# Recurrence: the two directions of a head pair as one product with a block-diagonal T

## The chip, the core and the metric

The kernel runs on one NeuronCore of a Trainium2 chip. The metric is the device time of one execution in microseconds (us), taken as the median of several runs. The engines, by the names of the profile, are PE (TensorE: products, with PEld for its weight loads), DVE (VectorE), ACT (ScalarE), POOL (GpSimd) and SP (SyncE, which here only issues DMAs).

## The reference, cut to what matters

One layer over 512 latent and 256 context tokens of width 1024: a modulated norm, an input projection into a recurrent mixer and a gating MLP, their merge, then 32 experts of which each token takes four. The change lies in the recurrent mixer (RWKV-7, 8 heads of 64, both directions). Per direction and head a 64x64 state goes through the tokens:

```python
def step(S, inp):
    r_t, w_t, k_t, v_t, a_t, b_t = inp
    sa = jnp.einsum('bhvk,bhk->bhv', S, a_t)
    S = S * w_t[:, :, None, :] + sa[..., None] * b_t[:, :, None, :] + v_t[..., None] * k_t[:, :, None, :]
    return S, (jnp.einsum('bhvk,bhk->bhv', S, r_t) if emit else None)
...
for d, rev in enumerate((False, True)):
    ...
    S_c, yc = wkv_scan(S0, rc, dc[d]['w'], dc[d]['k'], vc, dc[d]['a'], dc[d]['b'], rev, ctx_out)
    ...
    _, yl = wkv_scan(S_c, rl, dl[d]['w'], dl[d]['k'], vl, dl[d]['a'], dl[d]['b'], rev, True)
```

The context scan starts from zero, the latent scan from its last state; the two directions are summed for the latent tokens.

## The kernel before

**Chunks.** The recurrence isn't run token by token. Tokens are taken in 12 chunks of 64 (4 of context, 8 latent), and heads in 4 pairs p = 0 to 3, so there are 48 steps n = 12 p + i. In a step both directions (d = 0 forward, d = 1 backward) and both heads of the pair (par = 0, 1) are computed. Within a chunk the term sa of a token depends on those before it; this triangular system is solved ahead, once for each chunk, and its inverse T (64x64 for each direction and head) is stored in TT, a tile of 128x24x64: partitions 0 to 63 hold direction 0, partitions 64 to 127 direction 1, and column block 8 sb + 4 par + i % 4 is that of a chunk and head.

**Ahead of the chain.** For the next pair, while this one runs, `pre` (L682 to L724) makes decayed keys and queries, `solve_ab` (L770 to L775) the matrices of the systems, `solve_sub` (L792, L793, on DVE) solves their 32x32 blocks, and `solve_join` joins them (L816 to L824 on PE) and writes the last parts of TT (L825 on ACT, L826 on DVE). The dictionary `todo` in `rwkv` says after which step each of these parts is written into the program. They share the PSUM tag "pre" with two buffers, as `pre_bonus` and `readout` do.

**A step.** `chain_prep(p, i)` prepares operands that don't depend on the state: keys scaled on ACT (L846), turned on PE (L847) and copied back (L848, BKt), the values turned (L852) and copied into one half of UV (L853, L854), queries put into a zero-padded tile on ACT (L869, ARz), masked products with the keys (L873 on PE, L875 on DVE). Then up to two units of `fill` come, each six products of 128x128 by 512 columns (L1094) of the merge gates, which have nothing to do with the recurrence. Then `chain(p, i)`: products L893 and L896 into PSUM (tag "ch", two buffers), copy to Xs on DVE (L898), the product with T (L903), its result copied into the other halves of UV, on ACT (L904) for direction 0 and on DVE (L905) for direction 1; from UV the new state (L914 on PE, L918 or L920 on DVE, with the decayed old state from L911 on POOL), and for latent chunks the output (L927, L931, then L936 or L938 into the tile ysum). UV has two buffers, used in turn.

**The gates.** Each of 16 gates is four units of fill; FILLA gives the steps 2, 1, 1, 2, 1, 1, ... units. A gate ends with a tanh on ACT (L1099) into gt, L1100 on POOL, and for the last eight a product on POOL (L1104) with ybi, a tile of the pool W2 with one buffer, loaded by SP (L1089, L1090); then a store (L1102 or L1105). gt has one buffer.

**The readout.** After the last step of a pair `readout` (L940 to L969) centres ysum with a product (L950, L951), squares it on ACT (L953) into sq, sums that (L955), takes a root on ACT (L956) and reciprocals on DVE (L958), and scales ysum (L962 to L964 on POOL in the first three pairs). sq has the tag "gsq" with one buffer of its own.

**Order.** Each engine works through its own queue in order. In this part the framework plans the queues: it goes by the order of the program and by when operands and buffers are free, so that an instruction may stand ahead of ones that come before it in the program. The experts (from some 720 us on) keep an order written out by hand.

Of the kernel before, what the change touches and what calls it, by code (L numbers as in the profile page):

```python
# [7 lines left out]
F32 = mybir.dt.float32  # L8
# [147 lines left out]
class K:  # L156
# [671 lines left out]
    def chain_prep(self, p, i):  # L828

        nc = self.nc  # L830
        W = self.W2
        G = self.P[p]
        sb = i // 4
        AR, BK = G["AR", sb], G["BK", sb]
        ch = (i % 4, 3 - i % 4)
        S = G["step", i] = {}
        gc = 3 - i if sb == 0 else 15 - i
        S["f"] = f = (G["F"][:, 0, i + 1:i + 2], G["F"][:, 1, gc:gc + 1]) if i < 11 else None
        bk = S["BKt"] = W.tile([128, 2, 128], F32, name="BKt", bufs=2)
        uv = S["UV"] = self.UV[i % 2]  # L840
        pt = self.psC.tile([128, 4, 128], F32, name="prep")
        if f:

            bf = W.tile([128, 2, 128], F32, name="BKf", bufs=1)
            for d in range(2):
                nc.scalar.activation(bf[:, d, :], BK[:, d, ch[d], :], AF.Copy, scale=f[d])  # L846
                nc.tensor.transpose(pt[:, d, :], bf[:, d, :], self.ident)  # L847
            nc.scalar.copy(bk, pt[:, 0:2])  # L848
        for d in range(2):

            t = self.tok0(sb, d) + 64 * ch[d] + 64 * d
            nc.tensor.transpose(pt[:, 2 + d, :], G["v"][:, t:t + 128], self.ident)  # L852
        nc.scalar.copy(uv[64:128, 0], pt[64:128, 2])  # L853
        nc.scalar.copy(uv[0:64, 1], pt[0:64, 3])  # L854
        mm0 = self.psC.tile([128, 2, 512], F32, name="mm")
        if sb == 0:
            AK = S["AK"] = W.tile([128, 2, 64], F32, name="AK")
            for par in range(2):
                r = slice(64 * par, 64 * par + 64)
                nc.tensor.matmul(mm0[64:128, par, 0:64], BK[r, 0, ch[0], 64:128], AR[r, 0, ch[0], 0:64], start=True, stop=True)  # L860
                nc.tensor.matmul(mm0[0:64, par, 0:64], BK[r, 1, ch[1], 0:64], AR[r, 1, ch[1], 0:64], start=True, stop=True)
            nc.vector.tensor_mul(AK, mm0[:, :, 0:64], self.cst[:, C_MSKC:C_MSKC + 64].rearrange("p (a t) -> p a t", a=1).to_broadcast([128, 2, 64]))
        else:

            AZ = W.tile([128, 2, 2, 128], F32, name="ARz", bufs=1)
            a0, a1 = AR[:, 0, ch[0], :], AR[:, 1, ch[1], :]
            both = bass.AP(tensor=a0.tensor, offset=a0.offset, ap=[list(a0.ap[0]), [a1.offset - a0.offset, 2], [1, 128]])
            for par in range(2):
                nc.scalar.activation(AZ[:, :, par, :], both, AF.Copy, scale=self.cst[:, C_BLK + 64 * par:C_BLK + 64 * par + 1])  # L869
            mm = mm0[:, 0, :].rearrange("p (d a t) -> p d a t", d=2, a=2)  # L870
            MM = S["MM"] = W.tile([128, 2, 2, 128], F32, name="MM", bufs=2)
            for d in range(2):
                nc.tensor.matmul(mm[:, d].rearrange("p a t -> p (a t)"), BK[:, d, ch[d], :], AZ[:, d].rearrange("p a t -> p (a t)"), start=True, stop=True)  # L873
            msk = self.cst[:, C_MSK:C_MSK + 256].rearrange("p (d a t) -> p d a t", d=2, a=1)
            nc.vector.tensor_mul(MM, mm, msk.to_broadcast([128, 2, 2, 128]))  # L875

    def chain(self, p, i):
        nc = self.nc
        W = self.W2
        G = self.P[p]  # L880
        sb = i // 4
        AR, TT = G["AR", sb], G["TT"]
        S = G["step", i]
        ch = (i % 4, 3 - i % 4)
        St, Sn = self.S[(i + 1) % 2], self.S[i % 2]
        uv, bk = S["UV"], S["BKt"]
        xp = self.psC.tile([128, 2, 64], F32, name="ch", bufs=2)
        for par in range(2):
            for d in range(2):

                r = slice(0, 128) if sb > 0 else slice(64, 128) if d == 0 else slice(0, 64)
                ak = S["AK"][r, par, :] if sb == 0 else S["MM"][:, d, par, 0:64]
                nc.tensor.matmul(xp[64 * d:64 * d + 64, par, :], ak, uv[r, d, 64 * par:64 * par + 64], start=(par == 0), stop=(i == 0 and par == 1))  # L893
        if i > 0:
            for d in range(2):
                nc.tensor.matmul(xp[64 * d:64 * d + 64].rearrange("p a b -> p (a b)"), AR[:, d, ch[d], 0:64], St[:, d, :], start=False, stop=True)  # L896
        Xs = W.tile([128, 2, 64], F32, name="Xs", bufs=2)
        nc.vector.tensor_copy(Xs, xp)  # L898
        up = self.psC.tile([128, 2, 64], F32, name="ch", bufs=2)
        for par in range(2):  # L900
            for d in range(2):
                r = slice(64 * d, 64 * d + 64)
                nc.tensor.matmul(up[r, par, :], TT[r, 8 * sb + 4 * par + i % 4, :], Xs[r, par, :], start=True, stop=True)  # L903
        nc.scalar.copy(uv[0:64, 0].rearrange("p (b v) -> p b v", b=2), up[0:64])  # L904
        nc.vector.tensor_copy(uv[64:128, 1].rearrange("p (b v) -> p b v", b=2), up[64:128])  # L905
        if i < 11:
            f = S["f"]
            if i > 0:
                FS = W.tile([128, 2, 128], F32, name="FS", bufs=2)
                for d in range(2):  # L910
                    nc.gpsimd.tensor_scalar(FS[:, d, :], St[:, d, :], f[d], None, op0=OP.mult)  # L911
            sp = self.psC.tile([128, 2, 128], F32, name="ch", bufs=2)
            for d in range(2):
                nc.tensor.matmul(sp[:, d, :], bk[:, d, :], uv[:, d, :], start=True, stop=True)  # L914
            for par in range(2):
                r = slice(64 * par, 64 * par + 64)
                if i == 0:
                    nc.vector.tensor_copy(Sn[r, :, r], sp[r, :, r])  # L918
                else:
                    nc.vector.tensor_add(Sn[r, :, r], sp[r, :, r], FS[r, :, r])  # L920
        if sb > 0:
            MM = S["MM"]
            if i == 4:
                G["y"] = W.tile([128, NLAT], F32, name="ysum")
            yp = self.psC.tile([128, 2, 64], F32, name="ch", bufs=2)
            for d in range(2):
                nc.tensor.matmul(yp[:, d, :], St[:, d, :], AR[:, d, ch[d], 64:128], start=(d == 0), stop=False)  # L927
            for d in range(2):
                for par in range(2):
                    r = slice(64 * par, 64 * par + 64)  # L930
                    nc.tensor.matmul(yp[r, d, :], uv[:, d, r], MM[:, d, par, 64:128], start=False, stop=(d == 1))  # L931
            for d in range(2):
                t = self.tok0(sb, d) + 64 * ch[d] - 256
                o = G["y"][:, t:t + 64]
                if sb == 1:
                    nc.scalar.copy(o, yp[:, d])  # L936
                else:
                    nc.vector.tensor_add(o, o, yp[:, d])  # L938

    def readout(self, p):  # L940

        nc = self.nc
        W = self.W2
        G = self.P[p]
# [4 lines left out]
        ps = self.psR.tile([128, 512], F32, name="pre", bufs=2)  # L949
        nc.tensor.matmul(ps, blk, y, start=True, stop=True)  # L950
        nc.vector.scalar_tensor_tensor(y, ps, -1.0 / 64, y, op0=OP.mult, op1=OP.add)  # L951
        sq = W.tile([128, 512], F32, name="gsq")
        nc.scalar.activation(sq, y, AF.Square)  # L953
        ps = self.psR.tile([128, 512], F32, name="pre", bufs=2)
        nc.tensor.matmul(ps, blk, sq, start=True, stop=True)  # L955
# [16 lines left out]
    def rwkv(self, fill):  # L972
        nc = self.nc
        todo = {}
        self.UV = []
        for j in range(2):
            t = self.W2.tile([128, 2, 128], F32, name=f"UV{j}")
            nc.gpsimd.memset(t, 0.0)
            self.UV.append(t)
        for q in range(1, 4):  # L980
            a = 12 * (q - 2)
            work = [(at, lambda q=q, sb=sb: self.pre(q, sb)) for sb, at in enumerate(PRE if q > 1 else PRE1)]
            work.append((S_END, lambda q=q: self.pre_end(q)))
            work += [(S_AB + sb, lambda q=q, sb=sb: self.solve_ab(q, sb)) for sb in range(3)]
            work += [(S_SUB + i, lambda q=q, i=i: self.solve_sub(q, 31 * i // NSUB, 31 * (i + 1) // NSUB)) for i in range(NSUB)]
            work += [(S_SUB + NSUB + h, lambda q=q, h=h: self.solve_join(q, h)) for h in range(2)]
            work.append((S_BON, lambda q=q: self.pre_bonus(q)))
            for at, f in work:
                todo.setdefault(a + at, []).append(f)
        for n in range(48):  # L990
            p, i = n // 12, n % 12
# [1125 lines left out]
```

## Time and profile before

| | us |
|---|---|
| runs | 1987.66, 1989.9, 1995.83 |
| median | 1989.9 |
| profiled execution, device time | 1995.05 |
| its span, first to last instruction | 1993.3 |
| PE busy in the span | 1903.4 (95%) |
| DVE busy | 1703.8 (85%) |
| ACT busy | 1246.2 (63%) |
| POOL busy | 567.5 (28%) |
| mean granted clock of PE | 0.977 of 2.4 GHz |

The span is divided by the page into 40 slices of 49.8 us. The recurrence lies in slices 7 to 14, some 308 to 678 us. A product's time in the trace goes from its first column to the end of its way through the array, and consecutive products overlap; so an engine that the table calls busy may still have room. In the timeline a row may stand for several instructions of one line (x8), with the start of the first and the time they cover together.

### The profile page before, as it was taken

The page shows a single profiled execution, that of the slowest core. Times are in us where ns is not written, and L with a number is a line of the kernel's source. Part 1 is how long each engine was busy: PE and PEld are TensorE (multiplying, and loading weights), DVE is VectorE, ACT ScalarE, POOL GpSimd, SP SyncE. Part 2 cuts the span into 40 slices and gives each one's busy share as a digit, 9 for nine tenths or more (in the row PEclk, how much of TensorE's full clock was granted, in tenths as well). Part 3 has the DMA queues.
Part 4 walks back from the last instruction along what each step waited for, and adds up shares of the span by engine and source line. Part 5 has one row for each costly group of instructions (what it writes and reads, how often), then busy time and mean ns, then how long its engine had stood idle before and what let it go on. Part 6 is the DMA issues. An engine that isn't in the chain of part 4 may idle for free.

```text
span 1993.3 us, 28998 instructions
## 1 busy us (share of the span) xinstructions
PE 1903.4 (95%) x11136; PEld 1485.9 (75%) x11136; DVE 1703.8 (85%) x1764; ACT 1246.2 (63%) x1441; POOL 567.5 (28%) x423
## 2 busy tenths in 40 slices
PE   7999988989999898999999999999999999999996
PEld 4767766767676688777888887887878878878874
DVE  5755785877776568899999999999999999999996
ACT  4522535454545435777777777777777777777773
POOL 0000516343433364522131131221321311312212
PEclk9999989998989998999999999999999999999998
DMA  9665223120112375999999999999999999999994
GB/s 323 207 202 191 88 94 116 41 81 20 50 43 72 126 246 206 340 354 359 375 364 360 368 367 367 369 365 375 367 359 373 367 363 369 364 371 372 347 383 141
DMA packets 153122, 530.58 MB, mean 266 GB/s; under 512 B 16112, under 2 KB 77296, under 8 KB 103825
## 3 DMA queue, kind: packets, MB, share of 16 engines
q1 hardware_dynamic: 140343, 495.85, 67.0%
q0 software_dynamic: 10272, 26.94, 5.8%
q10 hardware_dynamic: 2362, 5.87, 0.8%
q8 instruction: 90, 1.47, 0.3%
q14 instruction: 55, 0.45, 0.1%
HBM read 500.48 MB, written 36.08 MB: 269 GB/s over the span
## 4 chain that ended last, share of the span: by engine, by line
PE 69%; DVE 7%; issue 3%; POOL 3%; DMA 2%; ACT 1%; SPq 0%; POOLq 0%; DVEq 0%; ACTq 0%
PE dn L1505 6%; PE dn L1504 6%; PE dn L1509 6%; PE up L1504 6%; PE up L1505 6%; PE up L1509 6%; PE gp L1505 6%; PE gp L1504 6%; PE gp L1509 6%; PE fill L1094 2%; PE b L1594 1%; PE b L1553 1%; PE mm L873 1%; PE ch L914 1%; PE acc L166 1%
## 5 line engine op out<-in xcount | busy, mean ns | idle before, releaser
L1493 DVE TENSOR_TENSOR wl<-raw,wh 128x2048 fp32r<-128x2048 f32 x384 | 928.0, 2461 | 1.9 <-issue 1.0
L1487 ACT CAST wh<-raw 128x2048 fp32r<-128x2048 f32 x384 | 721.3, 1905 | 80.7 <-PE gp L1505 65.7
L1540 POOL DMA_INDIRECT xg<-d_h,slots x30 | 35.1, 1171 | 687.0 <-PE b L1553 679.1
L1504 PE MATMUL dn<-wh,aH 128*128 128x512 f32 x512 | 208.3, 407 | 0.7 <-ACT aH L1597 0.7
L1505 PE MATMUL dn<-wh,aL 128*128 128x512 f32 x512 | 206.4, 403 | 0.3 <-DVE aL L1598 0.2
L1504 PE MATMUL up<-wh,xH 128*128 128x512 f32 x512 | 206.2, 403 | 0.0
L1504 PE MATMUL gp<-wh,xH 128*128 128x512 f32 x512 | 205.3, 401 | 0.0
L1505 PE MATMUL up<-wh,xL 128*128 128x512 f32 x512 | 203.0, 397 | 0.0
L1505 PE MATMUL gp<-wh,xL 128*128 128x512 f32 x512 | 202.9, 396 | 0.0
L1612 POOL TENSOR_TENSOR y<-y,mH 128x1024 f32<-128x1024 f32 x31 | 135.8, 4381 | 152.0 <-ACT y L1611 152.0
L1509 PE MATMUL dn<-wl,aH 128*128 128x512 f32 x512 | 140.5, 396 | 0.7 <-DVE wl L1493 0.7
L1509 PE MATMUL up<-wl,xH 128*128 128x512 f32 x512 | 139.7, 394 | 0.0
L1509 PE MATMUL gp<-wl,xH 128*128 128x512 f32 x512 | 139.4, 394 | 0.0
L1597 ACT CAST aH<-b 128x512 fp32r<-128x512 f32 x64 | 37.6, 587 | 144.1 <-PE b L1594 144.1
L1505 PEld LDWEIGHTS dn<-wh,aL 128*128 128x128 f32 x512 | 96.8, 189 | 32.6 <-DVE aL L1598 13.4
L1509 PEld LDWEIGHTS dn<-wl,aH 128*128 128x128 f32 x512 | 96.6, 189 | 24.1 <-DVE wl L1493 1.1
L1509 PEld LDWEIGHTS gp<-wl,xH 128*128 128x128 f32 x512 | 96.1, 188 | 23.6
L1509 PEld LDWEIGHTS up<-wl,xH 128*128 128x128 f32 x512 | 96.6, 189 | 22.7
L1504 PEld LDWEIGHTS up<-wh,xH 128*128 128x128 f32 x512 | 96.5, 189 | 22.6
L1505 PEld LDWEIGHTS up<-wh,xL 128*128 128x128 f32 x512 | 96.8, 189 | 21.6
L1505 PEld LDWEIGHTS gp<-wh,xL 128*128 128x128 f32 x512 | 96.4, 188 | 21.6
L1504 PEld LDWEIGHTS gp<-wh,xH 128*128 128x128 f32 x512 | 96.3, 188 | 21.4
(524 smaller groups left out, 3851.4 us busy)
## 6 DMA issues: line engine op xcount, KB each, us to landing
raw<-in_exp_w_gate_dram SPq DMA_DIRECT2D x128, 1024.0 KB, 7.6
raw<-in_exp_w_up_dram SPq DMA_DIRECT2D x128, 1024.0 KB, 10.1
raw<-in_exp_w_down_dram SPq DMA_DIRECT2D x128, 1024.0 KB, 7.5
raw<-in_w_ada_dram SPq DMA_DIRECT2D x32, 512.0 KB, 4.5
raw<-in_w_in_dram SPq DMA_DIRECT2D x24, 512.0 KB, 4.0
wa<-in_w_ada_dram SPq DMA_DIRECT2D x7, 1024.0 KB, 13.1
raw<-in_w_in_dram SPq DMA_DIRECT2D x6, 1024.0 KB, 5.3
raw<-in_w_o_dram SPq DMA_DIRECT2D x8, 512.0 KB, 5.7
```

Of the source, the lines that this page charges most:

```text
L166: return mm(ps, aH, bL, start=False, stop=last)
L873: nc.tensor.matmul(mm[:, d].rearrange("p a t -> p (a t)"), BK[:, d, ch[d], :], AZ[:, d].rearrange("p a t -> p (a t)"), start=True, stop=True)
L914: nc.tensor.matmul(sp[:, d, :], bk[:, d, :], uv[:, d, :], start=True, stop=True)
L1094: nc.tensor.matmul(ps, a[:, k, :], b[:, k, :], start=(n == 0), stop=(n == 23))
L1487: self.nc.scalar.copy(h, t)
L1493: self.nc.vector.tensor_sub(lo, t, h)
L1504: mm(ps[:, c, :], xH[:, k0 + kk, :], wh[:, cs], start=first and kk == 0, stop=False)
L1505: mm(ps[:, c, :], xL[:, k0 + kk, :], wh[:, cs], start=False, stop=False)
L1509: mm(ps[:, c, :], xH[:, k0 + kk, :], wl[:, cs], start=False, stop=last and kk == 1)
L1540: self.nc.gpsimd.indirect_dma_start(out=t, out_offset=None, in_=self.d_h2, in_offset=bass.IndirectOffsetOnAxis(ap=self.slots[:, e:e + 1], ...
L1597: nc.scalar.copy(aH, pt)
L1612: nc.gpsimd.tensor_mul(y, y, self.ga2)
```

## The change

At the head of `chain_prep` two copies on ACT take T of this chunk out of TT, one for each direction, and put it into a tile TZ of 128x2x128: direction 0 into rows and columns 0 to 63 of each head's 128x128 block, direction 1 into rows and columns 64 to 127. The rest of TZ is zero; two such tiles, used in turn like UV, are cleared on POOL once, at the start of `rwkv`. In `chain` the product with T is then one for each head, with weights of 128x128 and all 128 rows of Xs, where it was one for each head and direction with weights of 64x64. In `readout` the square sq takes the tag "ybi", and with it the one buffer that the gates load ybi into; "gsq" goes away.

```diff
@@ chain_prep
         uv = S["UV"] = self.UV[i % 2]
+        tz = self.TZ[i % 2]
+        for d in range(2):
+            r = slice(64 * d, 64 * d + 64)
+            t = G["TT"][r, 8 * sb + i % 4:8 * sb + i % 4 + 1, :]
+            t = bass.AP(tensor=t.tensor, offset=t.offset, ap=[list(t.ap[0]), [256, 2], [1, 64]])
+            nc.scalar.copy(tz[r, :, r], t)
         pt = self.psC.tile([128, 4, 128], F32, name="prep")
@@ chain
         up = self.psC.tile([128, 2, 64], F32, name="ch", bufs=2)
         for par in range(2):
-            for d in range(2):
-                r = slice(64 * d, 64 * d + 64)
-                nc.tensor.matmul(up[r, par, :], TT[r, 8 * sb + 4 * par + i % 4, :], Xs[r, par, :], start=True, stop=True)
+            nc.tensor.matmul(up[:, par, :], self.TZ[i % 2][:, par, :], Xs[:, par, :], start=True, stop=True)
@@ readout
-        sq = W.tile([128, 512], F32, name="gsq")
+        sq = W.tile([128, 512], F32, name="ybi")
@@ rwkv
+        self.TZ = []
+        for j in range(2):
+            t = self.W2.tile([128, 2, 128], F32, name=f"TZ{j}")
+            nc.gpsimd.memset(t, 0.0)
+            self.TZ.append(t)
```

## Rows read from the trace of the kernel before

**Rows 1.** Table by stage: stretch, length, busy us (records), clock, DMA share, GB/s.
```profile
308.00:678.00 370.00, 345.01 (x3386) 253.19 (x3384) 268.41 (x603) 189.25 (x529) 155.23 (x205) 0.95 0.18 56
338.00:355.00 17.00, 15.11 (x164) 11.64 (x163) 10.66 (x21) 7.58 (x28) 10.05 (x14) 0.80 0.22 63
438.00:461.00 23.00, 20.66 (x180) 14.45 (x180) 14.86 (x27) 9.71 (x31) 9.58 (x13) 0.63 0.22 70
```

**Rows 2.** View of line L904: duration min/median/max in ns, first and last start.
```profile
L904 ACT COPY UV<-ch x48: 240/258/259, 311.6 to 675.5; 64x128 f32<-64x128 f32 x48
```

**Rows 3.** Timeline of a step: start, us, engine, line, tiles, shape, count.
```profile
643.79 0.60 PE L873 MATMUL mm<-ARz,BK 128*128 128x256 f32 x2
...
644.32 0.45 PE L903 MATMUL ch<-Xs,TT 64*64 64x64 f32 x8
...
644.70 0.44 PE L847 MATMUL prep<-first,BKf 128*128 128x128 f32 x2
644.82 0.26 ACT L904 COPY UV<-ch 64x128 f32<-64x128 f32 x1 [0.29 <-PE ch L903]
...
644.98 0.60 PE L873 MATMUL mm<-ARz,BK 128*128 128x256 f32 x2
...
645.41 0.61 PE L914 MATMUL ch<-UV,BKt 128*128 128x128 f32 x4
...
645.85 0.56 PE L927 MATMUL ch<-AR,S 128*128 128x64 f32 x4
...
646.34 0.45 PE L931 MATMUL ch<-MM,UV 128*64 128x64 f32 x8
```

**Rows 4.** Views of lines L903, L927: weight loads, PE's idle time ahead of L903.
```profile
L903 PEld LDWEIGHTS ch<-Xs,TT x384: 128/135/224, 311.0 to 675.1; 64*64 64x64 f32 x192
...
  DVE Xs L898: 10.9, 17
...
L927 PEld LDWEIGHTS ch<-AR,S x128: 186/192/333, 351.2 to 675.6; 128*128 128x128 f32 x128
```

**Rows 5.** Groups by line, ACT, 308 to 678: busy us, mean ns, idle.
```profile
L846 ACT ACTIVATE BKf<-BK,F 128x128 f32<-128x128 f32 x85 | 30.2, 398 | 9.0 <-PE prep L847 8.9
```

**Rows 6.** Waits of ACT, 308 to 678 us: total us, times, longest.
```profile
ACT UV L904 <- PE ch L903: 15.1, 17, 2.9
```

**Rows 7.** Timelines of DVE and PE at the start of pair 2.
```profile
515.04 0.56 DVE L826 COPY TT<-pre 32x384 f32<-32x384 f32 x1 [1.21 <-ACT TT L825]
...
515.52 0.27 PE L903 MATMUL ch<-Xs,TT 64*64 64x64 f32 x1
```

**Rows 8.** Table by stage of tile pre alone: PE, PEld, DVE, ACT busy.
```profile
355.00:363.00 8.00, 3.34 (x20) 2.69 (x20) 1.32 (x2) 1.28 (x4) 1.00 0.31 98
363.00:405.00 42.00, 0.01 (x1) 0.00 (x0) 0.00 (x0) 0.98 (x4) 1.00 0.16 49
```

**Rows 9.** View of tile ybi: loads, products, time from issue to landing.
```profile
L1090 SPq DMA_DIRECT2D ybi<-d_yb x8: 377/424/1343, 304.0 to 659.7; - x8
L1104 POOL TENSOR_TENSOR gt<-gt,ybi x8: 1267/1271/2007, 522.5 to 675.4; 128x512 f32<-128x512 f32 x8
...
DMA to landing us min/median/max: 2.7/2.7/3.3
```

**Rows 10.** Timeline of POOL: first step, readouts of pairs 1 and 2.
```profile
303.70 0.57 POOL L978 MEMSET UV<- 128x256 f32 x2
...
535.64 1.29 POOL L962 TENSOR_TENSOR ysum<-ysum,gsq 128x512 f32<-128x512 f32 x1 [4.61 <-issue]
...
612.40 1.27 POOL L1104 TENSOR_TENSOR gt<-gt,ybi 128x512 f32<-128x512 f32 x1
...
626.53 1.26 POOL L962 TENSOR_TENSOR ysum<-ysum,gsq 128x512 f32<-128x512 f32 x1 [5.53 <-DVE UV L905]
```

**Rows 11.** Timeline of ACT behind the readout of pair 2.
```profile
627.67 0.60 ACT L1099 ACTIVATE gt<-fill 128x512 f32<-128x512 f32 x1
```

**Rows 12.** Table by stage of line L1094 (fill) alone: PE and PEld busy.
```profile
628.00:635.00 7.00, 2.19 (x6) 0.97 (x6) 1.00 0.08 29
```

## The prediction

> **What bounds the kernel now.** I first read the page's busy shares by slice, to find the stretch that the change touches, and then the table by stage for it. From 308 to 678 us TensorE is busy 345.01 of 370 us, VectorE 268.41, ScalarE 189.25 [rows 1]. The 48 steps of the recurrence fill this stretch: their copies L904 start between 311.6 and 675.5 us [rows 2], so a step takes (675.5 - 311.6) / 47 = 7.7 us. The change adds nothing to the 1,300 us behind it. That looks like a stage bound by TensorE, but the timeline of one light step [rows 3] says something else: the reader should see there a chain that goes from engine to engine (products L893 and L896, Xs, product L903, copies L904 and L905, product L914, the sum into S), with other products queued in between. A product's span contains its way through the array, so a full row of TensorE isn't a full array. The light steps are bound by chain and queue together, the others by VectorE's solve and by waits between all engines.
>
> **The product.** The four products of L903 become two. In the trace each fp32 product has two records, so 8 become 4. The reader should see in [rows 3] that the eight last 0.45 us together, less than four full ones: products of d=0 and d=1 lie side by side in different quarters of the array, and merging them takes away little. The nearest row for the new form is L927 (128x128 weights, 64 columns, four records): 0.56 us. Four records of L914 (128 columns) take 0.61, which is the upper end.
>
> Getting in and out also counts. From the start of L873 to L903 it is 644.32 - 643.79 = 0.53 us, from L873 to the full-array L914 645.41 - 644.98 = 0.43, so the new product may start 0.10 earlier where TensorE's queue is late. The next full-array product follows L903 after 0.38 us. The new product holds it back 0.44 (L914 to L927), and in the best case 0.39 (L927 to L931 takes 0.49, of which I subtract the same 0.10 for the narrower form) [rows 3].
> - Where TensorE waits for Xs (17 of 48 steps [rows 4]) there is no early start: 0.11 to 0.16 us more. By the row of the same form, 17 x 0.11 = +1.9 us.
> - In the other 31 steps the result comes 0.01 to 0.06 later: +0.3 us by the low end.
> - What queues behind comes earlier: 0.53 + 0.38 = 0.91 against 0.43 + 0.39 to 0.44 = 0.82 to 0.87, that is 0.04 to 0.09 a step. At most 48 x 0.09 = -4.3 us, and nothing where the chain is late. I take 31 x 0.05 = -1.5 us.
>
> A load of 128 columns costs 0.192 us by its median, one of 64 columns 0.135 [rows 4]. The Trainium skill (TensorE: Matmul & The Clock Gate, LDWEIGHTS) says that a load's time goes with its columns, not with its rows. By that rule filling a tile with zeros buys rows for nothing and pays for columns, which speaks against this change; the difference in the trace, 0.057 us, agrees with its 64 / 1.2 = 53 ns. By its figure the four wide loads would add 4 x 53 ns x 48 = 10 us (an estimate) if nothing hid them, against the 2.2 us of my two terms; what the rows make of such a case is a rival below.
>
> **The copies on ScalarE.** Two copies of 64x128 a step, 96 in all. The nearest row is L904, same shape from PSUM, 0.240 to 0.259 us [rows 2]; the other end is L846, 128x128 from SBUF with a scale, 0.398 [rows 5]. I take 0.26: 96 x 0.26 = 25 us more work, and ScalarE goes from 189 to 214 of 370 us. The copies need only TT, finished well before in all but three steps, and a tile that the product two steps back has released; so they can run a step ahead. Behind them in ScalarE's order stand BKf (L846), BKt (L848), the two v copies, ARz (L869) and L904; TensorE waits for BKf, BKt, ARz and UV. What hides them is ScalarE's idle half: in 17 steps it sat idle until L903 ended, 15.1 us in all [rows 6]. Without that cover it is the whole 25 us. I price the meeting of the two: an instruction finds a copy under way with a chance of 25/370 = 7% and waits half of 0.26 us, 0.009 us; with four waited-for groups a step, 48 x 4 x 0.009 = +1.7 us. Ends: 0 and +25.
>
> **The start of a pair.** Three times the first step waits for the solve. Before head pair 2 the last piece of TT is written from 515.04 to 515.60, and L903 has its first product at 515.52, on the half that ScalarE wrote; the last piece is in use at once [rows 7]. Now a copy of 0.26 and a hand-off lie between; when both come late, two. 0.3 to 0.6 us, I take 0.5: 3 x 0.5 = +1.5 us. At the first pair there is time.
>
> **The buffer.** The readout's square loses its own buffer and takes that of ybi, which the gates load (L1089, L1090). TZ needs 2 x 1 KB a partition, the old gsq 2 KB, so no room is gained or lost. Who gets the buffer first? The trace answers for another tag: pre(2, 1) stands behind solve_join(1, 0) in the program and uses the same loads as pre(2, 0), which is done by 363 us. Still no "pre" buffer is written from 363 to 405 us (0.01 us of TensorE, against 3.34 in the 8 us before) [rows 8], while the join waits for the solve. So buffers of a tag are given out in the program's order: squares of pairs 0 and 1, then ybi 0 to 3, square 2, ybi 4 to 7, square 3. The early load at 304.0 goes; ybi 0 may only follow the square's last use, POOL's L962 at 535.64 + 1.29 = 536.93 [rows 10], and land 2.7 us later, so its product moves from 522.5 [rows 9] to about 540. Its tile gt is then free by some 544; products of gates are (675.4 - 522.5) / 7 = 22 us apart [rows 9], so this is hidden, just. In pair 2 it isn't: the product at 612.40 moves behind L962 (626.53 + 1.26) [rows 10] and the load, to about 631; after its 1.27 us and a store (taken as the load's 2.7) gt is free at about 635, and the tanh of the gate behind, at 627.67 now [rows 11], waits for it. The fill behind that tanh did six records, 2.19 us, between 628 and 635 [rows 12]. They move. 0 to 7 us; I take 1.5. SP's queue holds behind the waiting load only stores and w_out_rwkv, needed later.
>
> The two memsets on POOL go behind those of UV, 0.57 us for two, and some 4 us before POOL is next at work [rows 10]: nothing; without this gap 0.57 us, once.
>
> **Sum.** 1.9 + 0.3 - 1.5 + 1.7 + 1.5 + 1.5 = +5.4 us. Profiled: 1995.05 + 5.4 = 2000.4. That execution is 5.15 us above the median of the runs, 1989.9; on the median I forecast 1995.3, rounded 1995.
>
> **Rivals.**
> - *Slower, ScalarE becomes late.* The chain's L904 and the prepared operands wait behind the copies. For it: in 31 steps ScalarE was not idle when L903 ended [rows 6]. Against it: half of its time is idle, and TensorE, which it serves, hardly is [rows 1]. It decides from the point where the copies are issued between L903 and L904 in most steps: 0.26 to 0.52 us a step, 12 to 25 us, 2002 to 2015, middle 2009.
> - *Slower, the buffer goes to whoever is ready first.* Then the load at 304 keeps it until the product at 522, the square of pair 0 waits for gate 8, and the next pair's fifth step for the tile ysum. By FILLA 22 of the 36 units that end with gate 8 are then done; TensorE would run 14 units of 6 records alone, at 2.19 / 6 = 0.365 us [rows 12] 31 us without a chain, of which later steps may win half back, having less fill: 15 us, about 2010. Against it: [rows 8].
> - *Slower, wide weights in the path.* If each of four loads shows its additional 0.057 us [rows 4], 0.23 us a step, 11 us: 2001. Against it: the row of L927 has them in it and is 0.11 longer.
> - *Faster, TensorE is the bound.* Then 4.3 us come from the shorter occupation, and the fuller array may keep the clock: from 438 to 461 us, while solve_ab's 64x64 products run, it is granted 0.63 of 2.4 GHz on the mean, so it spends most of the time at 1.2, and 180 records pass in 23 us; at the rate of the same work from 338 to 355 (164 in 17, granted 0.80) it would be 18.7 [rows 1]. With as much in the next pair, 4.3 + 2 x 4.3 = 13 us: 1977, one from the lower end. Against it: only some three steps fall in each stretch.
> - *The change does not do what it says.* It halves the products and not their time, since they ran side by side already; that is in my sum.
>
> **Chances.** Forecast 0.53 (1985 to 2000 by itself); ScalarE 0.14; buffer 0.09; wide weights 0.07; faster 0.17. Half a per cent, 10 us, is about what a measurement can tell here. So faster 0.17, same 0.53, slower 0.30. The order in the queues is planned anew and can shift light steps either way, which the bounds must hold too: 1976 to 2014 leaves out part of the faster case and the end of ScalarE's.
>
> **What would show it.** The new product's four records at 0.56 us; copies near 0.26 us; L873 to product 0.43; ScalarE at 214 us; no ybi load before 537; the product at 612 behind 630. I'm wrong if ScalarE's copies stand between product and L904 step after step, if the stretch from 308 to 678 changes by more than 10 us, or if a term outside it moves.

## The result, and the profile after

| | before | after |
|---|---|---|
| median of five runs, us | 1989.99 | 2007.3 |
| lowest to highest, us | 1987.66 to 1995.83 | 2005.45 to 2012.24 |
| profiled execution: device time / span, us | 1995.05 / 1993.3 | 2007.14 / 2005.4 |
| mean granted clock of PE, of 2.4 GHz | 0.977 | 0.970 |

The ratio is 1.0081, 95% interval 1.0063 to 1.0098: the change makes the kernel slower by 0.8%, 17 us by the medians. That lies inside the range of 1976 to 2014 and 12 us above the forecast of 1995; the part on the prediction says how far the reasons for it held.

Up to L840 lines keep their numbers. Behind it those that matter here moved thus: the new copies are L846, BKf L852, Xs L904, the product L907, the copies into UV L908 and L909, the state's product L918, the turned values L858, the masked product L879, the square L957, POOL's product with it L966, fill L1104, tanh L1109, the product with ybi L1114.

**Where the time went.** The stretch from the first Xs to the last took 363.9 us before and 380.9 after, 17.0 more; what lies behind it got 3.9 shorter (1318.7 to 1314.8). So the stage is the place to look. These are tables by stage with the columns of [rows 1], the stage cut at each pair's first Xs, four pairs, before and then after:

```profile
310.70:408.00 97.30, 88.68 (x826) 67.19 (x826) 78.18 (x176) 51.38 (x149) 45.05 (x62) 0.96 0.22 69
408.00:512.60 104.60, 96.49 (x944) 70.28 (x944) 81.35 (x179) 52.50 (x146) 42.59 (x58) 0.92 0.16 51
512.60:609.00 96.40, 90.98 (x921) 66.69 (x919) 75.94 (x172) 49.38 (x138) 40.75 (x49) 0.93 0.16 48
609.00:674.60 65.60, 63.52 (x660) 45.34 (x658) 30.24 (x74) 32.78 (x93) 21.40 (x29) 1.00 0.15 47
```

```profile
309.70:407.80 98.10, 89.80 (x772) 70.22 (x772) 76.43 (x174) 56.13 (x167) 44.63 (x62) 0.93 0.20 63
407.80:516.60 108.80, 100.38 (x903) 76.90 (x902) 82.22 (x181) 59.11 (x172) 42.65 (x58) 0.89 0.17 54
516.60:619.00 102.40, 94.93 (x871) 71.52 (x872) 77.37 (x171) 54.91 (x161) 41.55 (x49) 0.88 0.15 46
619.00:690.60 71.60, 67.50 (x615) 50.51 (x614) 29.25 (x75) 39.01 (x117) 21.81 (x29) 0.93 0.15 46
```

The reader should compare three columns. PE has fewer records in every pair (772 for 826, and so on: four fewer a step, apart from how the rest falls) and yet is busy longer: 339.7 us in the four pairs before, 352.6 after, so that 12.9 of the 17.0 us are busy time and 4.1 are idle time (24.2 before, 28.3 after). ScalarE gained 5 to 7 us in each pair, which are the copies. And the clock fell in every pair. TensorE's clock has two levels, so a mean of 0.93 over 98.1 us means 2 x 0.07 x 98.1 = 13.7 us at 1.2 GHz. Summed over the stage from the trace's clock records that is 37.5 us before and 71.7 after. Half of the additional 34.2 us is 17.1, as much as the whole loss. That the two agree so well is in part chance, since the idle time grew too and the products became fewer.

That products take nearly twice as long at the lower level can be read in rows. Fill products of 512 columns that follow each other without a gap, in a stretch at each level of the kernel after:

```profile
491.04 0.63 PE L1104 MATMUL fill<-hH,wh 128*128 128x512 f32 x1
...
491.46 0.63 PE L1104 MATMUL fill<-hH,wl 128*128 128x512 f32 x1
...
660.98 0.40 PE L1104 MATMUL fill<-hH,wh 128*128 128x512 f32 x1
661.21 0.40 PE L1104 MATMUL fill<-hH,wl 128*128 128x512 f32 x1
```

One every 0.42 us at 1.2 GHz and every 0.23 at 2.4. The Trainium skill (TensorE: Matmul & The Clock Gate, HAM oscillation — how this bites in real kernels) puts the cost of throttled time at half of it and has waits for data between groups of products bring it on. These rows come near the half; on the waits the runs here show less, as the next part and copies_end_mm tell.

**A wait and the clock behind it.** Step 20 has a stall of the same kind in both kernels. Tables by stage, one stretch with the stall and one behind it, before and then after:

```profile
486.00:489.00 3.00, 1.52 (x17) 1.02 (x15) 2.87 (x5) 0.58 (x2) 1.29 (x1) 1.00 0.10 19
490.00:493.00 3.00, 3.00 (x29) 2.00 (x29) 2.73 (x10) 0.97 (x4) 1.29 (x2) 1.00 0.23 67
```

```profile
487.00:490.00 3.00, 1.07 (x10) 0.83 (x10) 2.91 (x4) 1.84 (x6) 1.44 (x1) 1.00 0.20 71
491.00:494.00 3.00, 3.00 (x8) 2.31 (x7) 2.27 (x8) 0.00 (x0) 1.33 (x2) 0.50 0.29 87
```

The stall in the timelines, before and then after:

```profile
486.07 0.40 PE L1094 MATMUL fill<-hH,wl 128*128 128x512 f32 x1
487.95 0.49 PE L914 MATMUL ch<-UV,BKt 128*128 128x128 f32 x2 [1.48 <-DVE UV L905]
```

```profile
485.93 2.51 POOL L189 TENSOR_TENSOR wl<-raw,wh 128x1024 fp32r<-128x1024 f32 x1
...
486.20 0.60 ACT L846 COPY TZ<-TT 64x128 f32<-64x128 f32 x2
486.26 2.46 DVE L792 TENSOR_TENSOR tmpu<-Mu,Tu 128x256 f32<-128x256 f32 x1
...
488.75 0.29 DVE L909 COPY UV<-ch 64x128 f32<-64x128 f32 x1
...
489.10 0.49 PE L918 MATMUL ch<-UV,BKt 128*128 128x128 f32 x2 [1.93 <-DVE UV L909]
```

VectorE's solve instruction lasts 2.46 us where others of nearly its size take 0.41 to 0.42, and it does so while POOL is at work on L189; the copy L909 is queued behind it, and TensorE waits for that, 1.93 us where it was 1.48. Before, five fill products stood between the product with T and the wait (the last at 486.07); after, the planner had put five ahead of the step, and one was left here. In the stretch behind, the clock is 1.00 before and 0.50 after, from 490.6 to 494.0: 0.45 us more of waiting was followed by 3.4 us at the lower level, which by the half takes a further 1.7. One such place doesn't show that the longer wait decided it. In step 14 of the kernel after, TensorE waits 2.17 us until 437.1 and the clock stays up until 442.8; before, a wait of 1.81 us in step 8 is followed by no fall.

**The new operations.** Views of L907, L846 (min/median/max ns, first and last start), then waits of ACT in the stage, then DVE's row for the solve's Dg, before and after (L774 in both):

```profile
L907 PEld LDWEIGHTS ch<-Xs,TZ x192: 186/192/338, 310.2 to 691.3; 128*128 128x128 f32 x192
...
  DVE Xs L904: 9.9, 9
```

```profile
L846 ACT COPY TZ<-TT x96: 284/296/306, 303.5 to 682.3; 64x128 f32<-64x128 f32 x96
```

```profile
ACT UV L908 <- PE ch L907: 18.2, 18, 2.8
```

```profile
L774 DVE SCALAR_TENSOR_TENSOR Dg<-pre,cst,Dg 128x128 f32<-128x128 f32 x18 | 6.3, 348 | 7.2 <-ACT Dg L773 6.9
```

```profile
L774 DVE SCALAR_TENSOR_TENSOR Dg<-pre,cst,Dg 128x128 f32<-128x128 f32 x18 | 6.2, 349 | 12.5 <-ACT Dg L773 12.3
```

And a light step, to be laid beside [rows 3]:

```profile
662.65 0.60 PE L879 MATMUL mm<-ARz,BK 128*128 128x256 f32 x2
663.09 0.55 PE L907 MATMUL ch<-Xs,TZ 128*128 128x64 f32 x4
663.48 0.39 PE L858 MATMUL prep<-first,i_v 128*128 128x128 f32 x2
```

The product starts 0.44 us behind L879 (0.53 before), the next full-array product follows it after 0.39 (0.38), and it lasts 0.55.

**The buffer.** The view of ybi, then POOL and ACT behind the readout of pair 2, and fill there (table by stage of L1104 alone), to be laid beside [rows 9 to 12]:

```profile
L1100 SPq DMA_DIRECT2D ybi<-d_yb x8: 338/380/424, 543.4 to 675.8; - x8
```

```profile
635.29 1.27 POOL L966 TENSOR_TENSOR ysum<-ysum,ybi 128x512 f32<-128x512 f32 x1 [4.49 <-ACT BKf L852]
...
642.15 1.26 POOL L1114 TENSOR_TENSOR gt<-gt,ybi 128x512 f32<-128x512 f32 x1
...
647.70 0.60 ACT L1109 ACTIVATE gt<-fill 128x512 f32<-128x512 f32 x1
```

```profile
628.00:640.00 12.00, 3.44 (x13) 1.92 (x11) 1.00 0.17 48
640.00:652.00 12.00, 1.25 (x2) 0.53 (x2) 0.57 0.34 115
```

No ybi is loaded before 543, gate 12's product moves from 612.40 to 642.15, the next tanh from 627.67 to 647.70, and behind that wait TensorE has two fill records in 12 us, at a mean granted clock of 0.57.

### The profile page after: what moved, and what is told of

It reads as the page before. It is cut to its first block, busy times and chain, and to the rows that moved or that the text cites. A ratio compares the mean times of both kernels' runs of the same rounds, so it can differ in the third digit from the quotient of the medians.

```text
span 2005.4 us, 28717 instructions
## 1 busy us (share of the span) xinstructions
PE 1911.9 (95%) x10944; PEld 1501.8 (75%) x10944; DVE 1703.7 (85%) x1764; ACT 1270.9 (63%) x1537; POOL 569.2 (28%) x425
## 4 chain that ended last, share of the span: by engine, by line
PE 69%; DVE 7%; issue 4%; POOL 3%; DMA 2%; ACT 1%; POOLq 0%; SPq 0%; ACTq 0%; DVEq 0%
PE dn L1515 6%; PE dn L1514 6%; PE dn L1519 6%; PE up L1514 6%; PE up L1515 6%; PE up L1519 6%; PE gp L1515 6%; PE gp L1514 6%; PE gp L1519 5%; PE fill L1104 3%; PE b L1604 1%; PE b L1563 1%; PE ch L918 1%; PE mm L879 1%; DVE tmpu L792 1%
## 5 line engine op out<-in xcount | busy, mean ns | idle before, releaser
L1519 PEld LDWEIGHTS dn<-wl,aH 128*128 128x128 f32 x512 | 96.7, 189 | 23.0
L1515 PEld LDWEIGHTS gp<-wh,xL 128*128 128x128 f32 x512 | 96.4, 188 | 21.7
```

Of the source, the lines that this page charges most:

```text
L1515: mm(ps[:, c, :], xL[:, k0 + kk, :], wh[:, cs], start=False, stop=False)
L1519: mm(ps[:, c, :], xH[:, k0 + kk, :], wl[:, cs], start=False, stop=last and kk == 1)
```

## The experiments

The expectations name the theories by letters: B, the buffer that the readout shares with the gates; A, the copies on ScalarE; P, the product itself; C, TensorE's time at 1.2 GHz; Q, the order that the planner makes anew. Ratios are to the kernel before on the same chip, with 95% intervals. This table has the profiled execution of each, in us: a pair from its first Xs to the next pair's, and its time at 1.2 GHz, from the trace's clock records (2 x (1 - clock) x length of rows like those above).

| | ratio | pair 0 | pair 1 | pair 2 | pair 3 | stage |
|---|---|---|---|---|---|---|
| before | 1 | 97.3 / 6.8 | 104.6 / 17.1 | 96.4 / 13.7 | 65.6 / 0 | 363.9 / 37.5 |
| before_square_in_mm | 0.9994 | 95.6 / 3.4 | 104.7 / 17.1 | 96.4 / 13.7 | 65.3 / 0 | 361.9 / 34.1 |
| buffer_alone | 1.0018 | 96.9 / 6.8 | 104.7 / 17.1 | 98.8 / 17.1 | 69.2 / 6.8 | 369.6 / 47.8 |
| after (profile above) | 1.0081 | 98.1 / 13.7 | 108.8 / 23.9 | 102.4 / 23.9 | 71.6 / 10.2 | 380.9 / 71.7 |
| change_again | 1.0087 | 98.5 / 13.7 | 108.9 / 27.3 | 99.5 / 17.1 | 72.2 / 13.7 | 379.1 / 71.7 |
| square_in_mm | 1.0044 | 96.9 / 10.2 | 108.8 / 23.9 | 103.7 / 30.7 | 64.4 / 0 | 373.8 / 64.9 |
| copies_end_mm | 1.0076 | 98.8 / 13.7 | 110.6 / 30.7 | 103.0 / 27.3 | 66.7 / 6.8 | 379.0 / 78.5 |
| copies_alone | 1.0033 | 98.1 / 6.8 | 107.7 / 23.9 | 100.0 / 13.7 | 70.1 / 6.8 | 375.9 / 51.2 |
| no_copies | 1.0042 | 99.6 / 17.1 | 103.0 / 18.4 | 106.1 / 31.0 | 67.7 / 5.3 | 376.4 / 71.7 |
| pool_mm | 0.9970 | 96.7 / 10.2 | 103.6 / 17.1 | 92.9 / 3.4 | 63.7 / 0 | 357.0 / 30.7 |
| fill_moved_mm | 1.0025 | 99.1 / 3.4 | 93.6 / 6.8 | 103.1 / 20.5 | 70.4 / 0 | 366.2 / 30.7 |
| fill_moved_before | 1.0046 | 102.6 / 13.7 | 94.1 / 10.2 | 101.8 / 17.1 | 74.4 / 13.7 | 373.0 / 54.6 |
| warm_before | 1.0116 | 112.9 / 13.7 | 104.1 / 0 | 93.1 / 3.4 | 68.7 / 3.4 | 378.9 / 20.5 |
| warm_change | 1.0166 | 106.1 / 6.8 | 115.6 / 23.9 | 104.8 / 17.1 | 68.2 / 3.4 | 394.7 / 51.2 |

Each row is one execution, and executions of one kernel differ: those of copies_alone reach from 1993.84 us at a mean granted clock of 0.979 to 2010.15 at 0.975.

**The buffer alone.** The kernel before, with only this line changed:

```diff
-        sq = W.tile([128, 512], F32, name="gsq")
+        sq = W.tile([128, 512], F32, name="ybi")
```

> The kernel before, with one edit of the change alone: the readout's square takes the buffer of ybi. Theory B (the shared buffer holds back the gates of pairs 1 and 2, fill runs dry and the clock falls): 6 to 12 us over the kernel before, the stretch from first to last Xs 370 us or more against 363.9, more than 50 us at half clock in it against 37.5, the ybi product of gate 12 behind the third readout. Theory A (the copies on ScalarE) and theory P (the full-array product): no change, within 3 us.

Measured: 1.0018 (1.0007 to 1.0029), 3.6 us, less than the 6 to 12 that theory B expected. Pairs 0 and 1 stay as they were, pair 2 grows by 2.4 and pair 3 by 3.6. The waits are those that the prediction named: the product of gate 12 and the tanh behind it come later.

```profile
632.53 1.26 POOL L1104 TENSOR_TENSOR gt<-gt,ybi 128x512 f32<-128x512 f32 x1
```

```profile
639.05 0.60 ACT L1099 ACTIVATE gt<-fill 128x512 f32<-128x512 f32 x1
```

612.40 became 632.53, 627.67 became 639.05. Fill that isn't done then is done in the last steps, where nothing is left to hide it: from step 40 to 47 TensorE is busy throughout, before and then in this kernel.

```profile
639.40:674.60 35.20, 35.12 (x336) 26.44 (x335) 13.16 (x41) 16.10 (x55) 9.59 (x16) 1.00 0.06 17
```

```profile
642.30:679.30 37.00, 37.00 (x344) 27.90 (x344) 12.99 (x40) 15.89 (x55) 9.56 (x16) 1.00 0.10 30
```

Eight records more (six of them fill), at 0.23 us each, are the 1.8 us by which this stretch is longer.

**The square in another tile's buffers.** The change, but the square takes MM's two buffers, which the next steps need anyway, and ybi has its own again:

```diff
-        sq = W.tile([128, 512], F32, name="ybi")
+        sq = W.tile([128, 512], F32, name="MM", bufs=2)
```

> The changed kernel, but the square takes one of the two buffers of MM, which no step needs between a readout and the fifth step of the next pair, in place of ybi's. Theory B: half or more of the 17 us comes back, 1996 to 2000 us, and the half clock around 528 and 641 us is gone. Theories A and P: stays at 2005 to 2009.

Measured: 1.0044 (1.0030 to 1.0058), 8.8 us; the profile of pair 3 is back at 64.4 us with no time at 1.2 GHz. The time lies above the 1996 to 2000 us of theory B and below the 2005 to 2009 of A and P, and of the two stretches at 1.2 GHz that B named, the one at 641 us is gone and the one near 528 stays. By this run about half of the loss belonged to the buffer as this change uses it, in pair 3, and the other half to copies and product, in pairs 1 and 2; copies_end_mm below makes the buffer's half less certain.

The same line in the kernel before:

> The kernel before with the readout's square in one of MM's buffers and nothing else. If the 0.3% gain of the copies on GpSimd came from this buffer, 1985 to 1988 us here; if from the product with T, no change, within 3 us of the kernel before.

Measured: 0.9994 (0.9980 to 1.0009). The place in MM itself gives and costs nothing; square_in_mm is to be read against the kernel before as it is.

**The copies alone.** The change, with the four products of the kernel before, which read TT; TZ is filled and read by nobody:

```diff
-            nc.tensor.matmul(up[:, par, :], self.TZ[i % 2][:, par, :], Xs[:, par, :], start=True, stop=True)
+            for d in range(2):
+                r = slice(64 * d, 64 * d + 64)
+                nc.tensor.matmul(up[r, par, :], TT[r, 8 * sb + 4 * par + i % 4, :], Xs[r, par, :], start=True, stop=True)
```

> The changed kernel with its shared buffer and its copies into TZ, but the product with T in the four 64x64 products of before, which read TT; TZ is written and not read. Theory A: as slow as the changed kernel, 2004 to 2009. Theory P: falls to 2000 or below. Theory B says only that it stays 6 us or more over the kernel before, by the buffer.

Measured: 1.0033 (1.0010 to 1.0056). It holds the buffer's 0.18%, so the copies by themselves would be 0.15%, with an interval that holds zero; its profiled execution was 8 us above its median, so its row in the table is at the upper end. The row for Dg, with all the copies on ScalarE:

```profile
L774 DVE SCALAR_TENSOR_TENSOR Dg<-pre,cst,Dg 128x128 f32<-128x128 f32 x18 | 6.2, 347 | 6.4 <-ACT Dg L773 6.1
```

The wait is 6.1 us, no longer than the 6.9 without copies.

**The product alone.** The change without the two copies; T is left out of the computation, TZ stays zero, and the chain no longer waits for the solve:

```diff
-            nc.scalar.copy(tz[r, :, r], t)
+            pass
```

> The changed kernel without the copies: TZ stays zero, so T is left out of the computation; the two full-array products are done as in the change, with the shared buffer. Theory A: back to within 3 us of the kernel before but for the buffer. Theory P: as slow as the changed kernel, 2004 to 2009. Theory B: 6 us or more over the kernel before.

Measured: 1.0042 (1.0026 to 1.0058), so without any copy half of the loss is still there; 0.18% of it is the buffer's. The profiled execution spends as long at 1.2 GHz as the change (71.7 us), but elsewhere: pair 1 is short (103.0) and pair 2 the longest of all (106.1). Copies by themselves (0.15%), product by itself (0.24%) and buffer (0.18%) add to 0.57% where the change costs 0.81 to 0.87%; the intervals are too wide to say whether the parts simply add.

**The copies on GpSimd.** square_in_mm, with the copies moved off ScalarE:

```diff
-            nc.scalar.copy(tz[r, :, r], t)
+            nc.gpsimd.tensor_copy(tz[r, :, r], t)
```

> The change with the square in MM's buffer and the copies into TZ on GpSimd in place of ScalarE. Theory A (ScalarE's time): within 3 us of the kernel before. Theory C (half clock in the steps with solve_ab and pre): stays 6 to 10 us above it, with 60 us or more at half clock. Theory Q (the planner lays the queues out anew, and the new order is worse): anything, but light steps as fast as before and heavy ones not.

Measured: 0.9970 (0.9959 to 0.9982), 1986.33 us, faster than both kernels. The view of the copies, DVE's row for Dg, and pair 2 in the table by stage:

```profile
L846 POOL COPY TZ<-TT x96: 281/294/1197, 303.7 to 657.7; 64x128 f32<-64x128 f32 x96
```

```profile
L774 DVE SCALAR_TENSOR_TENSOR Dg<-pre,cst,Dg 128x128 f32<-128x128 f32 x18 | 6.1, 347 | 4.1 <-ACT Dg L773 3.8
```

```profile
510.10:603.00 92.90, 86.61 (x876) 66.50 (x875) 76.52 (x173) 49.22 (x137) 47.67 (x73) 0.98 0.17 50
```

The wait of the solve for ScalarE's Dg is 3.8 us, where it was 6.9 before and 12.3 after, and pair 2 runs at 0.98 of the full clock where it had 0.93 and 0.88. That would fit theory A with ScalarE late ahead of the chain and not in it; but copies_alone has the copies on ScalarE and waits 6.1 us, and fill_moved_mm has them there and waits 5.2. So the long wait belongs to some of the kernels with copies, not to the copies as such, and why this one gains is not shown.

**The same copies at another place.** square_in_mm, with the ScalarE copies written at the end of `chain_prep` instead of its head:

> The change with the square in MM's buffer and the same copies on ScalarE, but at the end of chain_prep in place of its head: the same work on the same engines, planned in another order. Theory A (ScalarE's time): as slow as with the copies at the head, 6 to 11 us over the kernel before. Theory Q (the planned order and the clock that comes with it): another time, by 5 us or more, and it goes with the half clock: about half a us for each us of it.

Measured: 1.0076 (1.0052 to 1.0101), with 78.5 us at 1.2 GHz. That is 0.3% above square_in_mm, though the two intervals overlap at their ends and the two ran on different chips. By the traces the new order is ScalarE's alone: in the stage TensorE, VectorE and GpSimd work through the same instructions in the same order as in square_in_mm, but for two places where a few neighbours are swapped, and each step has the same fill. TensorE is busy 355.6 us in place of 348.8 and idle 23.4 in place of 25.0. The same products thus took 6.8 us longer with 13.6 us more at 1.2 GHz: the half, in the cleanest form that the runs have, and what theory Q expected. Step 5 shows one place where the two part, square_in_mm first, each with the timeline and the table by stage behind it:

```profile
370.04 0.66 PE L907 MATMUL ch<-Xs,TZ 128*128 128x64 f32 x4 [1.71 <-DVE Xs L904]
...
370.70:374.00 3.30, 3.30 (x26) 2.64 (x24) 3.09 (x9) 2.39 (x9) 0.89 (x2) 1.00 0.00 0
```

```profile
370.62 0.67 PE L907 MATMUL ch<-Xs,TZ 128*128 128x64 f32 x4 [1.75 <-DVE Xs L904]
...
371.20:374.50 3.30, 3.30 (x14) 2.94 (x13) 2.29 (x7) 2.18 (x7) 0.00 (x0) 0.50 0.00 0
```

The wait is nearly the same, 1.71 and 1.75 us, and TensorE's work around it is the same; behind it the clock stays up in one and falls in the other. So neither the place of fill nor the length of a wait by itself decides, and the runs don't show what does.

**Fill moved.** More fill into the heavy steps, less into the light ones, in square_in_mm and then in the kernel before:

```diff
-FILLA = [2, 1, 1] * 16
+FILLA = [2, 1, 2, 2, 2, 2, 1, 1, 1, 1, 1, 0] * 3 + [2, 1, 1] * 4
```

> The change with the square in MM's buffer and the copies on ScalarE at the head; the units of fill are given to the heavy steps (FILLA 2, 1, 2, 2, 2, 2, 1, 1, 1, 1, 1, 0 for the first three pairs). Theory Q with the clock: where fill runs the clock stays up, so the half clock falls from 65 to under 45 us and the time to within 4 us of the kernel before. Theory A: 6 to 11 us over it, as without the move.

> The kernel before with the same FILLA, as the control of the run with the change: it has 37.5 us at half clock, so there is little to win; within 5 us of the kernel before. If it gains as much as the change does, the move says nothing about the change.

Measured: 1.0025 (1.0005 to 1.0044) and 1.0046 (1.0030 to 1.0062). The stage in the two, fill_moved_mm first:

```profile
312.00:678.20 366.20, 335.47 (x3156) 257.26 (x3156) 268.00 (x598) 211.20 (x615) 151.03 (x198) 0.96 0.17 54
```

```profile
310.30:683.30 373.00, 347.44 (x3344) 256.49 (x3344) 266.18 (x598) 185.57 (x523) 150.23 (x198) 0.93 0.17 53
```

The move helps the changed kernel and harms the one before, which was expected to stay within 5 us and lost 9. With 30.7 us at 1.2 GHz the one has a stage of 366, with 54.6 the other one of 373. The half explains little of the first: against square_in_mm it has 34.2 us less at 1.2 GHz and a stage only 7.6 shorter. With this placing the changed form is the faster one in the medians (1996.48 and 2002.59 us), though the intervals of the ratios overlap.

**TensorE kept at work.** Eight products of 128x128 by 384 columns are added in each of 13 heavy steps, written where nobody reads; first to the kernel before, then to square_in_mm:

```diff
+        if 12 * p + i in (3, 4, 5, 13, 14, 15, 16, 17, 24, 25, 26, 27, 28):
+            for _ in range(8):
+                nc.tensor.matmul(mm0[:, 1, 128:512], self.hH[:, 0, 0:128], self.hH[:, 1, 0:384], start=True, stop=True)
```

> The kernel before with eight added products of 128x128 by 384 columns in each of 13 heavy steps (3 to 5, 13 to 17, 24 to 28), into a part of the tile mm that nobody reads: 104 x 0.165 = 17 us of work for TensorE at full clock. Theory C: the half clock falls under 20 us, and the stretch grows by less than 10 us. Otherwise it grows by 10 to 20 us and the half clock stays near 37 us.

> The change with the square in MM's buffer and the same added products. Theory C: the half clock falls from 65 to under 25 us and the distance to the kernel with the added products and without the change is 3 us or less (it is 8.8 us without them). Theory Q: the distance stays at 6 to 12 us whatever the clock does.

Measured: 1.0116 (1.0081 to 1.0152) and 1.0166 (1.0149 to 1.0183). In the kernel before the time at 1.2 GHz fell from 37.5 to 20.5 us, while the stage grew by 15.0. In the changed one it only fell from 64.9 to 51.2, and the stage grew by 20.9. The two stay 12 us apart, so the expectation of C, that they would meet, fell. The test is weak: where in a heavy step the added products came was up to the planner, too.

**The change itself, again:**

> The changed kernel once more, on the chip and beside the runs of this call. If the parts found so far add up (buffer 3.6, copies and product with the square elsewhere 8.8): 0.6% over the kernel before, 11 to 14 us. The first comparison gave 0.81%.

Measured: 1.0087 (1.0068 to 1.0106), 17 us by the medians where 11 to 14 were expected, with the same 71.7 us at 1.2 GHz. Buffer_alone and square_in_mm add to 0.62%; their intervals reach the 0.81 to 0.87% of the whole, so the runs don't tell whether the two parts add or strengthen each other.

## Why the prediction was right and wrong

The time fell inside the range by luck more than by reasoning: the sum's terms came to +5.4 us, and what the loss of 17 goes with, TensorE's time at 1.2 GHz, is in none of them. The bounds were wide because the queues are planned anew, which the prediction said without a price.

- *The product* was right. In the light step shown, its entry was forecast at 0.43 and is 0.44, its hold on the next at 0.39 to 0.44 and is 0.39, its time 0.56 and is 0.55. TensorE waits for Xs 9 times instead of 17, though for nearly as long (9.9 us, 10.9 before) [rows 4]. That the halved products take no less time than the four was in the sum. The best proof is pair 3 of square_in_mm, which has the new product and all copies and no time at 1.2 GHz: 64.4 us against 65.6 before and 65.3 with the same square in the kernel before.
- *The rival of wide weights* fell: a load takes 0.192 us for 0.135 [rows 4], and the products behind and ahead of them don't move apart. The Trainium skill (TensorE: Matmul & The Clock Gate, LDWEIGHTS) has a load's time go with its columns, and the trace agrees that it grows with them. The prediction's price for this rival, and its estimate of 10 us, overlooked that four loads a step replace eight: by the medians all of them take 36.9 us (192 x 0.192) where they took 51.8 (384 x 0.135).
- *The copies* take 0.296 us and not 0.26, 28.4 us in all; ScalarE is busy 209.2 us in the stage (the four pairs), 186.0 before. POOL's clearing of TZ held the first of them 0.5 us, once, ahead of the first step. In the chain they are hidden as forecast: from the end of the product to the start of L908 the 48 steps together need 7.3 us, 6.8 before, and ScalarE still idles until the product in 18 steps, 17 before [rows 6]. What the sum left out is ScalarE's work for the solve. Its meeting of 0.009 us counted four groups of a step; the solve's Dg, which VectorE waits for, wasn't among them, and there 6.9 us became 12.3. That the copies do this isn't shown: with all of them on ScalarE the wait is 6.1 in copies_alone, and without any it is 8.6 in no_copies. Up to pool_mm in the table, kernels with copies on ScalarE have a pair 1 of 107.7 to 110.6 us in all five rows, those without them 103.0 to 104.7 in all five. In that pair TensorE's order is the same in after, change_again, square_in_mm and copies_end_mm, and nearly the same in before, buffer_alone and before_square_in_mm, so it is two orders against three. With fill moved the difference is gone (93.6 with copies, 94.1 without).
- *The rival "ScalarE becomes late"* gave 2002 to 2015, and 2007 lies in it. It is not borne out all the same: its mechanism was copies between product and L908, step after step, and the rows say no. A time that fits a rival doesn't prove the rival.
- *The start of a pair* costs nothing to speak of: from Xs to L908 the three first steps took 5.2, 4.9 and 6.8 us and take 5.0, 4.3 and 7.8. The 1.5 us were too much.
- *The buffer* went the way described, gate for gate, and not to whoever was ready first: the load at 304.0 is gone, the first is at 543. Its size was off: 3.6 us for 1.5 when it stands alone, and in pair 3 of the change 7.2 (71.6 against square_in_mm's 64.4 in the profiles; change_again has 72.2 and copies_end_mm 66.7). The step that failed is "they move": six fill records were taken as work that moves and finds room. There is no room in steps 40 to 47, where TensorE is full, and where the records are missing, behind 641 us, the clock fell.
- *The clock* is the term that the sum didn't have. It appears in the prediction only in the rival "faster", with the wrong sign: a fuller array would keep the clock. A fuller array didn't keep it; in step 20 it fell behind a longer wait, and how long TensorE waits there goes by where the planner puts fill. Take half of the time at 1.2 GHz off each stage of the table: before 345.2, before_square_in_mm 344.9, after 345.1, change_again 343.3, buffer_alone 345.7, square_in_mm 341.4, pool_mm 341.7, no_copies 340.6, copies_end_mm 339.8, copies_alone 350.3, fill_moved_mm 350.9, fill_moved_before 345.7. This is an estimate, since it takes all that time as filled with products. By it the change and its variants at full clock would lie between 5 us of gain and 6 of loss, where the sum had 5.4 of loss, and most of the loss of 17 would be the clock's.
- The sign that I had set for being wrong (the stage changes by more than 10 us) came true, by 17.0. The part behind the stage, which should not have moved, got 3.9 shorter; it lies between 1314.8 and 1319.5 us in all profiles here, and no run looks for a cause.

**What is shown and what isn't.** Shown, by making and undoing it: the buffer's part in pair 3 (its share of the whole, 0.18% alone and 0.05 to 0.43% when it is undone, is not settled), and that copies on GpSimd with the square in MM make the change a gain of 0.3%. Shown by the table: the stage is mostly longer where the time at 1.2 GHz is, and by square_in_mm and copies_end_mm that the same products take 6.8 us more with 13.6 us more of it. Not settled is why a given edit lengthens that time. ScalarE's copies may do it in pair 1; but no_copies has as much of it without them, and fill_moved_mm little of it with them. The planner lays out most of these edits' queues anew, and where fill falls moves the waits; yet copies_end_mm has square_in_mm's fill and nearly its waits, and 13.6 us more at 1.2 GHz. The clock is a link in this chain and not its beginning, and how much belongs to ScalarE, to the order and to chance the runs can't split.

## What to carry to other kernels

Where a framework plans the queues, an edit is not priced by its instructions alone: read the granted clock by stretches of the stage before and after, since two kernels with the same products in the same order differed here by 6.8 us of busy time. Before a difference is put down to one operation, look for a run that has the operation without the difference: the solve's longer wait for Dg looked like the work of the copies, and copies_alone has the copies without it. Before work is given to an engine that is half idle, it is worth trying another engine too; here that turned a loss of 0.4% into a gain of 0.3%. A buffer that is saved by sharing can hold back whoever comes second: here the first load of ybi came 239 us later, and the square in a tile that was idle at that time cost nothing measurable.

## What the runs showed of the hardware

- A copy of 64x128 in SBUF takes 0.296 us on ScalarE and 0.294 on GpSimd by their medians; GpSimd's longest is 1.197, ScalarE's 0.306.
- A VectorE instruction of two inputs from SBUF, 0.42 us otherwise, lasted 2.46 us while GpSimd worked on two inputs from SBUF for 2.51. The Trainium skill (SBUF — State Buffer, SBUF: two separate sides) calls the ports that the two share an exclusive lock held for the whole instruction; the timeline above agrees: the VectorE instruction started 0.33 us behind GpSimd's and ended 0.28 us behind its end.
- Merging four 64x64 products into two of the full array takes the entry behind a full-array product from 0.53 us to 0.44 and leaves the exit at 0.38 to 0.39; the merged product is no quicker in itself (0.55 us for 0.45).
- The same products in the same order took 6.8 us longer with 13.6 us more at 1.2 GHz (square_in_mm and copies_end_mm). Behind TensorE waits of 1.71 and 1.75 us, in the same step with the same TensorE work around them, the granted clock was 1.00 in one and 0.50 in the other.
